# Four feed-forward stages of a two-layer hybrid block: weight-block sums by adding transfers, low parts by VectorE

## The chip, the cores and the metric

The kernel runs on one core of a Trainium2 chip. A core has five engines with a queue of instructions each: TensorE (PE: matmuls, with PEld its weight loads), VectorE (DVE), ScalarE (ACT), GpSimd (POOL) and SyncE (SP, which here only starts transfers). Data lies in the on-chip SBUF (128 partitions), matmul results in PSUM banks of 512 fp32 columns, the weights in HBM. Transfers run on the core's sixteen DMA engines; SP starts plain ones, POOL starts those that add what they read to what stands at the destination.

The metric is the device time of one execution in microseconds (us); lower is better.

## The reference

Two layers with the width 1024 on 256 tokens. Each layer is feed-forward, mixer, feed-forward, with a residual and a layer norm behind each part; the mixer of the first layer is a hybrid of two recurrences, that of the second a sparse attention. The change touches the feed-forward alone:

```python
def swiglu(x, w_in, w_out):
    gate, up = jnp.split(x @ w_in, 2, axis=-1)
    return (jax.nn.silu(gate) * up) @ w_out
...
    for layer in range(DEPTH):
        i = layer // 2
        h = layer_norm(DEEPNORM_ALPHA * h + 0.5 * swiglu(h, ffn_w_in[layer, 0], ffn_w_out[layer, 0]),
                       ln_g[layer, 0], ln_b[layer, 0])
        ...
        h = layer_norm(DEEPNORM_ALPHA * h + mix, ln_g[layer, 1], ln_b[layer, 1])
        h = layer_norm(DEEPNORM_ALPHA * h + 0.5 * swiglu(h, ffn_w_in[layer, 1], ffn_w_out[layer, 1]),
                       ln_g[layer, 2], ln_b[layer, 2])
```

w_in is 1024 x 5632 (gate and up, 2816 columns each), w_out 2816 x 1024, all fp32. There are four feed-forward parts.

## The kernel before

**Two halves of each number.** A matmul runs on operands rounded to a shorter form (F32R). To keep fp32's accuracy each operand is split in a high part, the rounded value, and a low part, the value less the high part. A product is then three matmuls: high by high, low by high, high by low (`mm3`, line 818). Weights are split as they arrive (`halved`, line 676): ScalarE copies the 128x1024 tile to `whi`, VectorE subtracts it from `raw` into `wlo`. One tile is 512 KB.

**A feed-forward stage** (`ffn`, line 1044). The 2816 inner columns are done in eleven steps of 256. Steps 0 to 2 are plain products. The other eight steps are four *chunks* of 512 columns, each by seven products of half-size blocks instead of eight (`wide`, line 751): gate and up, the two halves of the 1024 rows and the two halves of the 256 tokens make 2 x 2 blocks; with sums of blocks on both sides seven products do. The token sums are made once a stage (`token_forms`, line 734). The sums on the weights' side are made in every chunk:

| product | weight block | made from |
|---|---|---|
| a | b11 | loaded |
| b | b11 + b12 | b, in b11's tiles |
| d | b11 + b12 + b22 | d, in b11's tiles |
| e | b12 + b22 | e, in b12's tiles |
| g | b22 | loaded |
| c | b21 | loaded |
| f | b11 + b12 + b22 + b21 | f, in b11's tiles |

A block is two tiles of 128x1024 (256 rows by 512 columns), so each of the four sums is two additions on VectorE (`add`, line 758), 128 in the program. A product is twelve matmuls of 512 columns into a bank named `ps` or `mp` (b and g).

**The second matrix.** As inner columns get ready, their rows of w_out are loaded (`weights_to`, line 1094, and `rows`, line 705) and multiplied into four banks `acc`, twelve matmuls for each 128 inner columns (`out_mm`, line 1061). These row terms are placed between the products of the chunks (`flush`, with the counts in `TERMS`). For rows 8, 10, ... 20 of each stage (`ADDED`, line 55; 28 in all) `rows` makes the low part without VectorE: ScalarE writes the negated rounded value to `wlo`, and a transfer started by POOL adds the weights from HBM to it once more.

**The order.** The kernel is written as a list of operations with their data dependences. A planner (`Plan.order`, line 352) turns the whole program, all six stages, into one fixed order for each engine before anything runs. It goes by a price for each operation, by the place in the list as priority, by a rate for the transfers, and by the tiles: 52 tiles of 4 KB a partition for everything, of which the stream "W" (weights: `raw`, `whi`, `wlo`) may hold 14 or 28. At run time an engine takes its instructions in that order and each waits for the semaphores of what it needs. All instructions bear the line 561, where the order is emitted, so groups are told apart by the names of their tiles.

**Stages in time.** Feed-forward 1 from 0 to about 187 us, the hybrid mixer to about 420, feed-forward 2 to about 600, feed-forward 3 to about 776, the sparse attention to about 900, feed-forward 4 to the end.

Of the kernel before, what the change touches and what calls it, by code (L numbers as in the profile page):

```python
# [10 lines left out]
F32R = mybir.dt.float32r  # L11
I32 = mybir.dt.int32
AF = mybir.ActivationFunctionType
OP = mybir.AluOpType
# [37 lines left out]

TERMS = ((0, 1, 1, 1, 1, 1, 1), (0, 0, 1, 1, 1, 1, 0), (0, 0, 1, 1, 1, 1, 0), (0, 0, 1, 1, 1, 0, 0))

ADDED = range(8, 22, 2)

STRANDS = ("mp",)
W_HYB, W_NSA = (60.0, 140.0, 25.0, 40.0, 15.0), (70.0, 60.0, 40.0, 20.0)
# [8 lines left out]
def H3(t, h):  # L67
    return t.rearrange("p (h t) -> p h t", h=h)
# [118 lines left out]
class Plan:  # L187
# [25 lines left out]
    def add(self, eng, fn, args, kw, alts=None):  # L213
        op = Op()
        op.eng, op.fn, op.args, op.kw, op.idx = eng, fn, args, kw, len(self.ops)
        op.prio = op.idx + self.base
        op.alts = alts
        op.deps, op.succ, op.alloc, op.nbytes = {}, [], None, 0
        if self.gate is not None:
            op.deps[self.gate] = True  # L220
        op.tiles = []
        writes, reads = [], []
        for n, a in enumerate(args):
            if isinstance(a, V):
                (writes if n == 0 else reads).append(a)
        for k, a in kw.items():
            if isinstance(a, V):
                (writes if k == "accum_out" else reads).append(a)
        seen = set()
        for a, w in [(a, False) for a in reads] + [(a, True) for a in writes]:  # L230
            t = a.t
            psum = t.space == "PSUM"
            if psum:
                p0, p1, at = 0, 128, None
            else:
                p0, p1, at = a.p0, a.p1, np.zeros(int(np.prod(t.shape[1:])), bool)
                at[a.ids] = True
            if not t.acc:
                assert w, (t.name, fn)
                t.order = op.idx  # L240
            keep = []
            held = False
            for x in t.acc:
                o, xw, a0, a1, xat = x
                hit = a0 < p1 and p0 < a1 and (at is None or bool((at & xat).any()))
                if hit and (w or xw) and o is not op:
                    op.deps[o.idx] = held = True
                if not (w and hit and p0 <= a0 and a1 <= p1 and (at is None or not (xat & ~at).any())) or o is op:
                    keep.append(x)
            keep.append((op, w, p0, p1, at))  # L250
            t.acc = keep
            if not held and id(t) not in seen:
                op.alloc = (op.alloc or []) + [t]
            if id(t) not in seen:
                seen.add(id(t))
                op.tiles.append(t)
                t.left += 1
        if TRACE is not None:
            TRACE(op, args)
        self.ops.append(op)  # L260
        return op
# [323 lines left out]
class K:  # L585
# [116 lines left out]

        return [(hi[:, e, :], lo[:, e, :]) for hi, lo in self.tiled(srcs, k) for e in range(hi.shape[1])]

    def rows(self, w, f, added=False):

        nc = self.nc
        raw = self.arrive(w[f])
        if not added:
            return self.halved(raw)  # L710
        hi, lo = self.m4(1024, "whi", "W", F32R), self.m4(1024, "wlo", "W", F32R)
        nc.scalar.activation(lo, raw, AF.Copy, scale=-1.0)
        nc.gpsimd.dma_start(lo, w[f], accum_op=OP.add)
        nc.scalar.activation(hi, raw, AF.Copy)
        return hi, lo

    def first_weights(self, w, n0, arrivals):

# [32 lines left out]
    def wide(self, w, n0, forms, gout):  # L751

        nc, V = self.nc, self.nc.vector

        def load(block):
            return [self.arrive(w[n0 + 2 * block + e]) for e in range(2)]

        def add(out, a):
            for e in range(2):
                V.tensor_tensor(out[e], out[e], a[e], OP.add)  # L760

        def product(bank, name, src, start, stop):
            ah, al = forms[name]
            on = {} if start and stop else dict(skip_group_check=True)
            mm = nc.tensor.matmul
            for e in range(2):
                wh, wl = (H3(t, 2) for t in self.halved(src[e]))
                for k in range(2):
                    n = 2 * e + k
                    mm(bank, ah[n], wh[:, k], start=start and n == 0, stop=False, **on)  # L770
                    mm(bank, al[n], wh[:, k], start=False, stop=False, **on)
                for k in range(2):
                    n = 2 * e + k
                    mm(bank, ah[n], wl[:, k], start=False, stop=n == 3, **on)

        r, q = self.bank("ps"), self.bank("mp")
        s, t, u, v = (H3(self.m4(1024, n, "F"), 2)[:, e] for n in ("su", "vg") for e in range(2))
        b11 = load(0)
        product(r, "a", b11, True, False)
        nc.scalar.activation(s, r, AF.Copy)  # L780
        yield
        b12 = load(1)
        add(b11, b12)
        product(q, "b", b11, True, False)
        yield
        b22 = load(2)
        add(b11, b22)
        product(r, "d", b11, False, False)
        nc.scalar.activation(t, r, AF.Copy)
        yield  # L790
        add(b12, b22)
        product(r, "e", b12, False, False)
        nc.scalar.activation(v, r, AF.Copy)
        V.tensor_tensor(v, q, v, OP.subtract)
        yield
        product(q, "g", b22, False, True)
        V.tensor_tensor(u, q, t, OP.subtract)
        yield
        b21 = load(3)
        p = self.bank("ps")  # L800
        product(p, "c", b21, True, True)
        V.tensor_tensor(s, p, s, OP.add)
        nc.scalar.activation(s, s, AF.Silu)
        V.tensor_tensor(u, s, u, OP.mult)
        yield
        add(b11, b21)
        product(r, "f", b11, False, True)
        nc.scalar.activation(t, r, AF.Silu)
        V.tensor_tensor(v, t, v, OP.mult)
        gh, gl = gout  # L810
        for b, g in enumerate((u, v)):
            pt = self.bank("mp")
            for f in range(4):
                nc.tensor.transpose(pt[:, f * P:(f + 1) * P], g[:, f * P:(f + 1) * P], self.ident)
            self.split(gh[:, :, b * P:(b + 1) * P], gl[:, :, b * P:(b + 1) * P], H3(pt, 4))
        yield
# [227 lines left out]
    def ffn(self, l, j, x, then, last=False):  # L1044
        nc = self.nc
        w_in = self.i['ffn_w_in'][2 * l + j]
        w_out = self.i['ffn_w_out'][l, j].rearrange("(k p) n -> k p n", p=P)
# [44 lines left out]
        terms, late, wos = [], [], []  # L1092

        def weights_to(n):
            while len(wos) < min(n, NF):
                wos.append(self.rows(w_out, len(wos), len(wos) in ADDED))

        def flush(most):
            for f, g in [terms.pop(0) for _ in range(min(most, len(terms)))]:
                weights_to(f + AHEAD)  # L1100
                out_mm(0, f, g, wos[f])
                if count[0, 0] > NF - LAG - (3 if last else 0):
                    late.append((f, g, wos[f]))
                else:
                    out_mm(1, f, g, wos[f])
# [3 lines left out]
        for s in range(NT, steps):  # L1109
            wg, wu = (self.col_tiles([w_in[8 + 4 * (s - NT) + 2 * n + e] for e in range(2)]) for n in range(2))  # L1110
            self.mark = len(self.plan.ops) - 1
            for e in range(2):
                f = 2 * s + e
# [8 lines left out]
                if s == NT and e == 0:  # L1122
                    forms = self.token_forms(x)
        weights_to(AHEAD)
        for n in range(CHUNKS):
            f0 = 2 * steps + 4 * n
# [76 lines left out]
    def rates(self, pg):  # L1203

        nc = self.nc
        self.ncs = self.sm([P, 48], "ncs")
        nc.scalar.activation(self.ncs, pg[:, :48], AF.Copy, scale=-1.0)
        pt = self.bank("mp")
        nc.tensor.transpose(pt[:48, :P], self.ncs, self.ident)
        rows = self.sm([48, P], "ncsT")  # L1210
        self.copy(rows, pt[:48, :P])
        self.caps.setdefault("rows", (1, "DRAM"))
        self.cum = self.plan.tile("rows", [48, P], F32, "rows", space="DRAM")
        nc.sync.dma_start(self.cum, rows)
# [1024 lines left out]
```

## Time and profile before

| | us |
|---|---|
| median of 3 runs | 1086.62 |
| lowest and highest | 1086.55, 1088.65 |
| the profiled execution | 1087.19 |
| its span, first to last instruction | 1085.5 |

The page gives the busy time of each engine, the transfers by queue (q1 is SP's, q0 POOL's), the chain of work that ended last, and the costliest groups of instructions. A group's row has the line, the engine, the operation, the tile written and those read, shapes and count; behind the bar the busy time in us, the mean of one in ns, and the idle time of the engine just before, with what ended it. The granted clock of TensorE was 0.995 of full speed. A matmul of 512 columns shows about 390 ns from its start to its end, but the next one starts 227 ns after it, since they are pipelined: the pace is read from the starts.

### The profile page before, as it was taken

What the parts mean: (1) busy time and instruction counts of PE and PEld (TensorE: products, weight loads), DVE (VectorE), ACT (ScalarE), POOL (GpSimd) and SP (SyncE); (2) the same over time, 40 slices, a digit from 0 to 9 for tenths busy, and PEclk for the clock granted to TensorE, in tenths of its full rate; (3) what the DMA queues carried; (4) which work ended last, traced back from release to release, by engine and by line L of the source; (5) the groups of instructions that cost most, each with busy time, mean ns of one, the idle gap of its engine ahead of it and who ended that gap; (6) DMA issues with size and microseconds to landing.
All of it is one profiled execution on the core that took longest, in us unless ns stands there. A gap on an engine that the chain in (4) does not pass through costs nothing.

```text
span 1085.5 us, 16212 instructions
## 1 busy us (share of the span) xinstructions
PE 1066.3 (98%) x5946; PEld 893.3 (82%) x5946; DVE 1010.9 (93%) x1453; ACT 725.9 (67%) x1155; POOL 70.7 (7%) x116
## 2 busy tenths in 40 slices
PE   8999999998999999999999999999999999999997
PEld 6788888897999788888888888888887778888886
DVE  7999999799979999999999999999978889999995
ACT  7767866368737774667866667678465778666780
POOL 1000000001001310000000000000001000000000
PEclk9999999999999999999999999999999899999999
DMA  8658768535433575367777736679563336457881
GB/s 330 231 196 256 221 233 284 179 135 182 140 115 99 194 269 180 117 230 251 215 229 254 257 125 215 235 241 303 189 214 98 92 123 216 152 188 236 255 231 41
DMA packets 65034, 215.71 MB, mean 199 GB/s; under 512 B 8301, under 2 KB 12218, under 8 KB 64954
## 3 DMA queue, kind: packets, MB, share of 16 engines
q1 hardware_dynamic: 60922, 199.98, 52.8%
q0 software_dynamic: 4032, 14.68, 7.2%
q8 instruction: 47, 0.77, 0.3%
q14 instruction: 33, 0.27, 0.1%
HBM read 211.86 MB, written 1.07 MB: 196 GB/s over the span
## 4 chain that ended last, share of the span: by engine, by line
PE 84%; DVE 12%; ACT 1%; DMA 1%; issue 1%; POOL 0%; SPq 0%; DVEq 0%; ACTq 0%
PE ps L561 39%; PE acc L561 31%; PE mp L561 14%; DVE wlo L561 2%; DVE cv L561 2%; DVE arena L561 1%; DMA raw<-in_ffn_w_in_dram 1%; DVE o L561 1%; DVE sw L561 1%; DVE x L561 1%; DVE y L561 1%; DVE qs L561 1%; DVE AT L561 0%; POOL arena L561 0%; DVE Y L561 0%
## 5 line engine op out<-in xcount | busy, mean ns | idle before, releaser
L561 ACT ACTIVATE whi<-raw 128x1024 fp32r<-128x1024 f32 (+1 forms) x435 | 436.8, 1052 | 104.0 <-DVE raw L561 85.4
L561 DVE TENSOR_TENSOR wlo<-raw,whi 128x1024 fp32r<-128x1024 f32 (+2 forms) x419 | 491.4, 1205 | 7.1 <-ACT whi L561 6.1
L561 PE MATMUL ps<-whi,x 128*128 128x512 f32 (+1 forms) x864 | 234.8, 390 | 0.3 <-ACT cv L561 0.3
L561 PEld LDWEIGHTS ps<-whi,x 128*128 128x128 f32 x864 | 156.7, 188 | 30.6 <-issue 1.5
L561 DVE TENSOR_TENSOR raw<-raw,raw 128x1024 f32<-128x1024 f32 x128 | 152.8, 1216 | 0.0
L561 PE MATMUL ps<-wlo,x 128*128 128x512 f32 (+1 forms) x432 | 127.1, 385 | 0.0
L561 PE MATMUL ps<-x,whi 128*128 128x256 f32 (+2 forms) x560 | 114.3, 312 | 4.0 <-ACT cv L561 2.4
L561 PEld LDWEIGHTS ps<-x,whi 128*128 128x128 f32 (+1 forms) x560 | 90.4, 188 | 11.4 <-ACT cv L561 3.8
L561 PE MATMUL acc<-whi,gh 128*128 128x512 f32 x253 | 99.3, 393 | 0.0
L561 PE MATMUL acc<-wlo,gh 128*128 128x512 f32 x253 | 99.0, 391 | 0.0
L561 PE MATMUL acc<-whi,gl 128*128 128x512 f32 x253 | 97.9, 390 | 0.0
L561 PEld LDWEIGHTS ps<-wlo,x 128*128 128x128 f32 x432 | 79.6, 188 | 15.3 <-issue 0.4
L561 PE MATMUL ps<-x,wlo 128*128 128x256 f32 (+1 forms) x344 | 80.0, 284 | 0.5 <-DVE wlo L561 0.5
L561 PE MATMUL acc<-whi,x 128*128 128x512 f32 x224 | 73.7, 405 | 2.3 <-DVE x L561 0.8
L561 PE MATMUL acc<-whi,g 128*128 128x512 f32 x192 | 63.3, 392 | 0.0
L561 POOL DMA_DIRECT2D wlo<-in_ffn_w_out_dram x28 | 24.4, 872 | 569.2 <-ACT wlo L561 391.3
L561 PEld LDWEIGHTS ps<-x,wlo 128*128 128x128 f32 (+1 forms) x344 | 58.1, 189 | 2.1 <-DVE wlo L561 0.7
L561 PEld LDWEIGHTS acc<-whi,gl 128*128 128x128 f32 x253 | 47.5, 188 | 9.8
L561 PEld LDWEIGHTS acc<-whi,gh 128*128 128x128 f32 x253 | 47.5, 188 | 9.5
L561 PEld LDWEIGHTS acc<-wlo,gh 128*128 128x128 f32 x253 | 47.5, 188 | 9.5
L561 PEld LDWEIGHTS acc<-whi,x 128*128 128x128 f32 x224 | 41.8, 189 | 11.8 <-ACT whi L561 2.1
L561 PE MATMUL mp<-whi,fhi 128*128 128x512 f32 x128 | 49.9, 390 | 0.0
(284 smaller groups left out, 1735.2 us busy)
## 6 DMA issues: line engine op xcount, KB each, us to landing
raw<-in_ffn_w_in_dram SPq DMA_DIRECT2D x174, 512.0 KB, 5.5
raw<-in_ffn_w_out_dram SPq DMA_DIRECT2D x88, 512.0 KB, 3.7
wlo<-in_ffn_w_out_dram POOLq DMA_DIRECT2D x28, 512.0 KB, 8.5
raw<-in_hyb_w_col_dram SPq DMA_DIRECT2D x28, 512.0 KB, 4.5
raw<-in_hyb_w_tok_dram SPq DMA_DIRECT2D x16, 512.0 KB, 7.8
raw<-in_hyb_w_out_dram SPq DMA_DIRECT2D x16, 512.0 KB, 3.7
raw<-in_nsa_w_tok_dram SPq DMA_DIRECT2D x8, 512.0 KB, 6.6
raw<-in_nsa_w_one_dram SPq DMA_DIRECT2D x8, 512.0 KB, 5.8
```

The costliest lines, as they stand in the source:

```text
L561: r = getattr(getattr(nc, eng), fn)(*[res(a) for a in args], **{k: res(a) for k, a in kw.items()})
```

## The change

The sums e and f of each chunk are no longer made by VectorE. A transfer started by POOL adds the block b22 from HBM to the tiles of b12 (sum e), and block b21 to the tiles of b11 (sum f). It is placed in the list as soon as the tile's earlier value isn't needed any more: e right behind sum b, f right behind product d. The blocks b22 and b21 are still loaded for their own products. In turn the second matrix's rows all get their low part from VectorE, and `ADDED` goes.

```diff
-ADDED = range(8, 22, 2)
+SUMS = ("e", "f")
...
-    def rows(self, w, f, added=False):
-
-        nc = self.nc
-        raw = self.arrive(w[f])
-        if not added:
-            return self.halved(raw)
-        hi, lo = self.m4(1024, "whi", "W", F32R), self.m4(1024, "wlo", "W", F32R)
-        nc.scalar.activation(lo, raw, AF.Copy, scale=-1.0)
-        nc.gpsimd.dma_start(lo, w[f], accum_op=OP.add)
-        nc.scalar.activation(hi, raw, AF.Copy)
-        return hi, lo
+    def rows(self, w, f):
+
+        return self.halved(self.arrive(w[f]))
...
-        def add(out, a):
+        def add(name, out, a, block):
             for e in range(2):
-                V.tensor_tensor(out[e], out[e], a[e], OP.add)
+                if name in SUMS:
+                    nc.gpsimd.dma_start(out[e], w[n0 + 2 * block + e], accum_op=OP.add)
+                else:
+                    V.tensor_tensor(out[e], out[e], a[e], OP.add)
...
         b12 = load(1)
-        add(b11, b12)
+        add("b", b11, b12, 1)
+        if "e" in SUMS:
+            add("e", b12, None, 2)
         product(q, "b", b11, True, False)
         yield
         b22 = load(2)
-        add(b11, b22)
+        add("d", b11, b22, 2)
         product(r, "d", b11, False, False)
+        if "f" in SUMS:
+            add("f", b11, None, 3)
         nc.scalar.activation(t, r, AF.Copy)
         yield
-        add(b12, b22)
+        if "e" not in SUMS:
+            add("e", b12, b22, 2)
         product(r, "e", b12, False, False)
...
-        add(b11, b21)
+        if "f" not in SUMS:
+            add("f", b11, b21, 3)
         product(r, "f", b11, False, True)
...
-                wos.append(self.rows(w_out, len(wos), len(wos) in ADDED))
+                wos.append(self.rows(w_out, len(wos)))
```

## The prediction

> **What bounds the kernel now.** I read the page first (engine shares, the chain of work that ended last), then the windows of the four feed-forward stages, then the chain inside one chunk, and last the waits.
>
> ```profile
> PE 1066.3 (98%) x5946; PEld 893.3 (82%) x5946; DVE 1010.9 (93%) x1453; ACT 725.9 (67%) x1155; POOL 70.7 (7%) x116
> PE 84%; DVE 12%; ACT 1%; DMA 1%; issue 1%; POOL 0%; SPq 0%; DVEq 0%; ACTq 0%
> ```
>
> TensorE (PE) is busy 98% of the span and holds 84% of the chain. VectorE (DVE), the engine that the change relieves, holds 12%. A share over the span doesn't say where, so the next view takes the stretch of the four chunks in each of the four feed-forward stages. Its columns are the length, the busy time of PE, weight loads, DVE, ACT and POOL, each with its count, then the granted clock, the DMA share and GB/s.
>
> ```profile
> 50.00:176.00 126.00, 126.00 (x573) 104.35 (x572) 124.56 (x124) 92.65 (x109) 6.19 (x7) 1.00 0.75 238
> 460.00:586.00 126.00, 126.00 (x573) 104.18 (x572) 123.12 (x124) 91.64 (x108) 6.09 (x7) 1.00 0.76 243
> 636.00:764.00 128.00, 128.00 (x581) 105.97 (x580) 125.82 (x145) 91.84 (x111) 6.02 (x7) 1.00 0.74 244
> 940.00:1068.00 128.00, 128.00 (x581) 105.79 (x580) 123.33 (x128) 88.02 (x104) 6.59 (x8) 1.00 0.68 210
> sum 508.00, PE 508.00 PEld 420.30 DVE 496.82 ACT 364.15 POOL 24.89; mean PE 127.00 PEld 105.08 DVE 124.21 ACT 91.04 POOL 6.22
> ```
>
> Two engines are full here: TensorE for 508.00 of 508.00 us, VectorE for 496.82. Which of them sets the pace? A matmul's end is modelled, so "busy" could hide waits of TensorE. The chain inside a chunk decides that: it lists starts, and a product is always twelve matmuls.
>
> ```profile
> 537.03 2.72 PE ps L561 x12
> 539.75 2.72 PE acc L561 x12
> 542.47 2.72 PE mp L561 x12
> 545.19 2.72 PE acc L561 x12
> 547.91 2.72 PE ps L561 x12
> 550.63 2.72 PE acc L561 x12
> 553.35 2.72 PE ps L561 x12
> ```
>
> Every twelve take 2.72 us, 0.227 us for each matmul, and the next twelve start in the same hundredth. Products of the first matrix (ps, mp) and row terms of the second (acc) alternate without a gap. The chain has nothing but PE in it. So TensorE sets the time of these stages at an even pitch, and VectorE, although full, keeps up. ScalarE does wait for VectorE's sums, 85.4 us of the 104.0 that it stands idle before the high copies (last two columns), and nobody behind it is late:
>
> ```profile
> L561 ACT ACTIVATE whi<-raw 128x1024 fp32r<-128x1024 f32 (+1 forms) x435 | 436.8, 1052 | 104.0 <-DVE raw L561 85.4
> ```
>
> **The change part by part.** The rows with the prices:
>
> ```profile
> L561 DVE TENSOR_TENSOR raw<-raw,raw 128x1024 f32<-128x1024 f32 x128 | 152.8, 1216 | 0.0
> 530.87 4.63 DVE L561 TENSOR_TENSOR wlo<-raw,whi 128x1024 fp32r<-128x1024 f32 x4
> L561 ACT ACTIVATE wlo<-raw 128x1024 fp32r<-128x1024 f32 x28 | 29.5, 1055 | 0.0
> q1 hardware_dynamic: 60922, 199.98, 52.8%
> q0 software_dynamic: 4032, 14.68, 7.2%
> DMA to landing us min/median/max: 5.4/8.5/11.2
> ```
>
> *Sums e and f.* There are 128 sums of blocks on VectorE: 4 stages x 4 chunks x 4 sums x 2 tiles. Half of them, 64, go. One lasts 1216 ns, but the starts of a run lie closer: (4.63 - 1.22) / 3 = 1.14 us. 64 x 1.14 = 73 us of VectorE go.
>
> *Low parts of the second matrix.* Rows 8, 10, ... 20 of each stage, 28 in all, lose the scaled copy on ScalarE (29.5 us) and the adding transfer, and get a subtraction of the same shape on VectorE: 28 x 1.14 = 32 us come back. Net VectorE: 73 - 32 = 41 us less, about 2.6 us for each of the 16 chunks. ScalarE: 29.5 us less.
>
> *What that is worth.* Nothing, by the chain above: the matmuls stay the same in number and shape, and they already follow each other at 0.227 us. The cover is TensorE itself. If it were gone, and VectorE set the pace, the 41 us would show (a rival below).
>
> *Adding transfers.* 28 go, 64 come: 36 more, 9 more in each stage. In the queue rows 28 transfers hold the sixteen DMA engines for 7.2% of 1085.5 us, so one takes 0.072 x 1085.5 / 28 = 2.79 us of all sixteen, where a plain load of the same 512 KB takes 0.528 x 1085.5 x 0.524 / 199.98 = 1.50 us. Nine more are 25.1 us a stage. Free DMA time in the four stretches: 126 x 0.25 = 31.5, 126 x 0.24 = 30.2, 128 x 0.26 = 33.3, 128 x 0.32 = 41.0 us. It fits, with 5 to 16 us left; the mean share rises to about 0.95, 0.96, 0.94 and 0.88. No row shows such a load kept up for 126 us. The nearest is the last chunk of the second stage, and the tight places are found by chunk:
>
> ```profile
> 50.00:80.00 30.00, 30.00 (x136) 24.85 (x135) 29.93 (x30) 19.65 (x24) 0.00 (x0) 1.00 0.63 205
> 460.00:490.00 30.00, 30.00 (x134) 24.76 (x133) 29.95 (x31) 18.06 (x21) 0.00 (x0) 1.00 0.62 211
> 554.00:586.00 32.00, 32.00 (x151) 26.46 (x150) 29.71 (x31) 26.69 (x33) 2.58 (x3) 1.00 0.95 299
> ```
>
> In 554 to 586 us the share is 0.95, three adding transfers are among it (the POOL count), and TensorE loses nothing. That row is nearest to what every chunk will look like, so I take the cost of the added traffic as zero; its other end, loads that come late, is priced under the rivals. The first chunks go from none to four transfers: 0.62 + 4 x 2.79 / 30 = 0.99.
>
> *The new wait.* The copy of e's and f's high part now waits for a transfer in place of a sum. On ScalarE the later copies are queued behind it, VectorE's low parts wait for those, and TensorE for both. Is there room? VectorE's list of the chunk around 520 us has the sums in the order b, b, e, d, d, e, f, f:
>
> ```profile
> 531.82 2.72 PE ps L561 x12
> 515.86 1.21 DVE L561 TENSOR_TENSOR raw<-raw,raw 128x1024 f32<-128x1024 f32 x1
> 535.42 2.35 DVE L561 TENSOR_TENSOR raw<-raw,raw 128x1024 f32<-128x1024 f32 x2
> ```
>
> The second b sum ends at 515.86 + 1.21 = 517.1; from then e's transfer may run. Product e is the ps that starts at 537.03, and its high copy takes 1.05 us, so the room is 537.03 - 1.05 - 517.1 = 18.9 us. For f, the block is free once product d (the ps at 531.82) has both halves, at the latest when it ends, at 534.5; product f starts at 553.35: 553.35 - 1.05 - 534.5 = 17.8 us. An adding transfer landed after 8.5 us in the median and 11.2 at worst. They now come in pairs, one sharing the engines with the other: 11.2 + 2.79 = 14.0 us, an estimate. That leaves 3.8 us, so I take 0. The other end is a pair that is late by one transfer in each chunk, 16 x 2.79 = 45 us; the 3.8 us speak against it, and a part of it stands among the rivals.
>
> *Issues and queues.* The row of the issues on POOL:
>
> ```profile
> L561 POOL DMA_DIRECT2D wlo<-in_ffn_w_out_dram x28 | 24.4, 872 | 569.2 <-ACT wlo L561 391.3
> ```
>
> It issues 64 such transfers of 0.87 us for 28; in these stages it has only the two powers of a layer norm to do besides (7 or 8 counts a stretch), and it is 93% idle: 0. SP's loads are the same, in another order. The tiles: no buffer is held longer than before, since b12 and b11 wait for their product anyway; the seven rows a stage need their low tile later: 0, or slightly below.
>
> *Order elsewhere.* The planner writes one order for the whole program, so the two mixers may come out in another order though no line of theirs changed. The sign is open. I take 0 and keep 4 us to both sides, 3% of the 12% x 1085.5 = 130 us that VectorE holds of the chain, which lie nearly all outside the feed-forward chunks.
>
> **Sum.** 0 (sums) + 0 (low parts) + 0 (transfers) + 0 (waits) on the profiled execution: it took 1087.19 us, its span is 1085.5, and the median of the runs shown is 1086.62. I forecast 1087, between the two.
>
> **The rivals.**
>
> *VectorE sets the pace after all: 1046 us.* For it: 496.82 of 508.00 us busy, and ScalarE's 85.4 us of waiting for sums. TensorE would then be stretched unseen, and the 41 us come off: 1087 - 41 = 1046. Against it: the even 2.72 us. The Trainium skill ("Perfetto Trace Analysis", Identifying the Most-Contended Engine) warns that matmul busy time is no measure of headroom and wants the busy share of the weight loads instead. By that rule the 420.30 of 508.00 us would promise up to 88 us of room; the trace doesn't bear it out here, since the starts of the matmuls leave none.
>
> *The freed engines help the mixers: 1083 us.* VectorE enters the hybrid and the attention stage with less backlog, and the order turns out better by the 4 us above. For it: VectorE's part of the chain lies there. Against it: that part is made of chains of small operations, not of weights.
>
> *The transfers press on the loads: 1096 us.* Place: chunks whose share reaches 1, that is the four first ones (0.99 by the sum above) and the last ones of the second and third stage (0.95 + 2.79 / 32 = 1.04). Mechanism: a load that is queued with a pair of adding transfers lands 2 x 2.79 = 5.6 us later.
>
> ```profile
> 507.08 0.80 SPq L561 DMA_DIRECT2D raw<-in_ffn_w_in_dram  x2
> 514.12 1.22 DVE L561 TENSOR_TENSOR raw<-raw,raw 128x1024 f32<-128x1024 f32 x1
> raw<-in_ffn_w_in_dram SPq DMA_DIRECT2D x174, 512.0 KB, 5.5
> ```
>
> A load issued at 507.08 lands after the median 5.5 us at 512.6, and the sum that wants it starts at 514.12: 1.5 us of slack. VectorE's new 2.6 us a chunk can make up for a stall. It decides beyond 1.5 + 2.6 = 4.1 us; the excess of 5.6 is 1.5 us a chunk, 6 x 1.5 = 9 us: 1096. For it: there is no chunk left with a slack share. Against it: the 0.95 chunk above lost nothing.
>
> *The order of the mixers turns out worse: 1091 us,* by the same 4 us.
>
> *The change doesn't do what it says,* say because the planner moves other work to VectorE: then the time is the same 1087, and it counts there.
>
> **How the numbers follow.** No change 0.45; loads pressed 0.25; mixers worse 0.07; mixers better 0.20; VectorE's pace 0.03. 0.2% is about what a measurement of this kernel can tell from no change, 2.2 us. Slower 0.32, same 0.45, faster 0.23. The range must reach the mixers' cases and nearly all of the pressed loads: 1081 (two us below 1083) to 1097. It leaves out the 0.03 of VectorE's pace and some 0.15 of tails. The likeliest case's own range is 1084.5 to 1089.
>
> **What would show it.** The sums on VectorE at 64 in place of 128, its low parts at 28 more of the 128x1024 form, 64 transfers on POOL; VectorE's busy time in the four stretches down by some 41 us while TensorE stays at 2.72 us for twelve: right. A DMA share of 0.95 with TensorE still even: the traffic fits. Wrong: pieces of DMA, ACT or DVE in the chain within 50 to 176 us and its like (loads pressed), or chunks that follow each other faster than now (VectorE's pace). If the four stretches are unchanged and the time moves, it comes from the mixers' order.

## The result, and the profile after

| | before | after |
|---|---|---|
| median | 1087.05 us (1086.55 to 1088.65, 4 runs) | 1095.51 us (1094.72 to 1097.92, 4 runs) |
| the profiled execution | 1087.19 us | 1094.72 us |
| its span | 1085.5 us | 1093.0 us |

The ratio after to before is 1.0079, with a 95% interval of 1.0059 to 1.0099. The kernel is slower by some 8 us, although VectorE and ScalarE both have less to do. The page of after:

```profile
PE 1069.3 (98%) x5946; PEld 892.5 (82%) x5946; DVE 976.8 (89%) x1421; ACT 700.7 (64%) x1123; POOL 101.5 (9%) x152
q0 software_dynamic: 9216, 33.56, 17.3%
PE 81%; DVE 11%; DMA 4%; issue 2%; ACT 1%; POOL 1%; SPq 0%; DVEq 0%; POOLq 0%; ACTq 0%
L561 DVE TENSOR_TENSOR raw<-raw,raw 128x1024 f32<-128x1024 f32 x64 | 76.9, 1216 | 0.2
raw<-in_ffn_w_out_dram SPq DMA_DIRECT2D x88, 512.0 KB, 5.7
raw<-in_ffn_w_in_dram POOLq DMA_DIRECT2D x64, 512.0 KB, 7.2
```

The change does what it says: 64 sums in place of 128 on VectorE, 64 adding transfers. VectorE is 1010.9 - 976.8 = 34.1 us less busy, ScalarE 25.2. But TensorE's part of the chain has gone down from 84% to 81%, and transfers hold 4% of it where they held 1%. The same four stretches as before, with the same columns:

```profile
50.00:176.00 126.00, 124.43 (x563) 102.19 (x563) 117.88 (x118) 89.91 (x105) 11.19 (x13) 1.00 0.92 278
460.00:586.00 126.00, 125.91 (x568) 103.12 (x566) 115.67 (x115) 87.35 (x104) 11.25 (x13) 1.00 0.93 279
636.00:764.00 128.00, 126.27 (x576) 104.08 (x574) 119.80 (x137) 88.96 (x107) 11.95 (x14) 1.00 0.89 267
940.00:1068.00 128.00, 127.17 (x581) 104.52 (x580) 117.30 (x120) 86.30 (x104) 12.19 (x14) 1.00 0.87 249
sum 508.00, PE 503.78 PEld 413.90 DVE 470.64 ACT 352.53 POOL 46.58; mean PE 125.94 PEld 103.48 DVE 117.66 ACT 88.13 POOL 11.64
```

The DMA shares are 0.92, 0.93, 0.89 and 0.87, close to the 0.95, 0.96, 0.94 and 0.88 that were foreseen. TensorE, which was busy for all of the 508.00 us, now has holes: 503.78. VectorE is less busy than before (470.64 for 496.82), so it is not full. What do the holes wait for? The waits of after (total us, times, longest):

```profile
DVE wlo L561 <- ACT whi L561: 29.8, 31, 3.4
ACT whi L561 <- DMA raw<-in_ffn_w_in_dram: 22.8, 21, 3.0
ACT whi L561 <- DMA raw<-in_ffn_w_out_dram: 14.0, 11, 2.9
PE mp L561 <- DVE vg L561: 4.1, 5, 1.6
```

And the three of them that the waits of before have:

```profile
ACT whi L561 <- DMA raw<-in_ffn_w_in_dram: 7.3, 5, 2.2
DVE wlo L561 <- ACT whi L561: 6.1, 11, 1.2
ACT whi L561 <- DMA raw<-in_ffn_w_out_dram: 1.4, 2, 1.0
```

Transfers now hold up ScalarE's high copies for 36.8 us in all (8.7 before). The one with w_out is plain loads of rows, and it has grown tenfold. The name with w_in could be plain loads or adding transfers. The profile's view of each queue's transfers tells them apart: for SP's plain loads it lists these copies as waiting for 42.8 us (all weights of all stages), for GpSimd's adding transfers it lists nobody. VectorE waits for those copies, 29.8 us (6.1), and TensorE waits for VectorE's `vg`, which it never did. The name `mp` covers two things, product g and the transposes at the end of a chunk, which read `vg` too; of the 4.1 us, 3.7 are product g's. These are the rows of the first kind of matmul of products b and g, before and after:

```profile
L561 PE MATMUL mp<-whi,fhi 128*128 128x512 f32 x128 | 49.9, 390 | 0.0
L561 PE MATMUL mp<-whi,fhi 128*128 128x512 f32 x128 | 51.0, 398 | 3.7 <-DVE vg L561 3.7
```

How these waits hang together is seen in the chain at one such hole (start, length, what), with the loads that stand in it at three other holes:

```profile
55.23 8.45 DMA raw<-in_ffn_w_out_dram
...
63.76 1.07 ACT whi L561
...
64.86 0.55 DVE wlo L561
65.40 0.60 issue
66.00 0.69 DVE vg L561
...
66.74 1.43 PE mp L561 x5
...
709.24 7.47 DMA raw<-in_ffn_w_out_dram
...
738.31 9.43 DMA raw<-in_ffn_w_in_dram
...
1014.21 8.64 DMA raw<-in_ffn_w_out_dram
```

Read it from the end. The `mp` at 66.74 is product g. It adds to the bank that holds product b, and VectorE must first have read b out of that bank: this is `vg`, the subtraction of b from e. Before it, ScalarE must have copied e out of its bank, into a tile that is named `vg` too. Both engines take their instructions in a fixed order, and high and low parts of other tiles stand ahead of these two. The timelines of ScalarE and VectorE at that place (start, busy time, in brackets the idle time before):

```profile
62.57 2.25 ACT L561 ACTIVATE whi<-raw 128x1024 fp32r<-128x1024 f32 x2 [2.73 <-DMA raw<-in_ffn_w_in_dram]
64.73 0.58 ACT L561 ACTIVATE vg<-ps 128x512 f32<-128x512 f32 x1
...
63.66 2.42 DVE L561 TENSOR_TENSOR wlo<-raw,whi 128x1024 fp32r<-128x1024 f32 x2 [1.69 <-ACT whi L561]
66.00 0.68 DVE L561 TENSOR_TENSOR vg<-mp,vg 128x512 f32<-128x512 f32 x1
```

ScalarE stands idle for 2.73 us until a load of w_in lands; it was issued at 50.24 and took 12.3 us. Its high copy is the first of the two at 62.57. The second is that of a row of the second matrix, whose load took 8.45 us and landed at 63.68, just as the first copy ended. Behind them stands the copy of e, which ends at 65.31. VectorE makes the two low parts of the same tiles, 1.69 us idle before the first, then `vg`, and behind `vg` waits TensorE. So two late loads, one of each matrix, stop product g, though neither the copy of e nor `vg` reads these tiles. The chain shows only the later of the two; by these times, as an estimate, either alone would have stopped product g for nearly as long. The holes that end near 722 and 1028 us lead back in the chain to loads of w_out that took 7.47 and 8.64 us, the one that ends near 753 to a load of w_in that took 9.43. The median from issue to landing went from 3.7 to 5.7 us for the loads of w_out and from 5.5 to 5.9 for those of w_in.

Where do the 7.5 us of the span come in? GpSimd computes a small power in each layer norm; its second one closes a stage. The last such row in after's timeline of GpSimd:

```profile
1087.09 0.92 POOL L561 TENSOR_TENSOR lnve<-lnve,mhalf 128x1 f32<-128x1 f32 x1 [11.57 <-DVE lnve L561]
```

These are the starts (us) of the same mark at the end of each stage, for both kernels and for three of the experiments below:

| end of | before | after | 64 columns | 330 GB/s plan | before, 330 GB/s plan |
|---|---|---|---|---|---|
| feed-forward 1 | 192.63 | 192.85 | 191.40 | 194.00 | 198.21 |
| hybrid | 429.93 | 431.33 | 429.89 | 430.56 | 437.46 |
| feed-forward 2 | 605.18 | 607.97 | 606.70 | 605.37 | 612.85 |
| feed-forward 3 | 779.89 | 784.45 | 781.76 | 781.06 | 787.92 |
| attention | 908.87 | 914.10 | 911.53 | 909.91 | 921.85 |
| feed-forward 4 | 1079.59 | 1087.09 | 1082.81 | 1080.45 | 1091.31 |

After against before: of 7.5 us, 5.65 come in the four feed-forward stages (0.2, 1.4, 1.8, 2.3) and 1.85 in the two mixers, whose code is the same.

### The profile page after: what moved, and what is told of

The parts are those of the page before. It is cut to its first block, busy times and chain, and to the rows that moved or that the text cites. A ratio compares the mean times of both kernels' runs of the same rounds, so it can differ in the third digit from the quotient of the medians.

```text
span 1093.0 us, 16286 instructions
## 1 busy us (share of the span) xinstructions
PE 1069.3 (98%) x5946; PEld 892.5 (82%) x5946; DVE 976.8 (89%) x1421; ACT 700.7 (64%) x1123; POOL 101.5 (9%) x152
## 4 chain that ended last, share of the span: by engine, by line
PE 81%; DVE 11%; DMA 4%; issue 2%; ACT 1%; POOL 1%; SPq 0%; DVEq 0%; POOLq 0%; ACTq 0%
PE ps L561 38%; PE acc L561 30%; PE mp L561 14%; DVE wlo L561 3%; DMA raw<-in_ffn_w_out_dram 2%; DMA raw<-in_ffn_w_in_dram 2%; DVE arena L561 1%; DVE cv L561 1%; ACT whi L561 1%; DVE sw L561 1%; POOL arena L561 1%; DVE qs L561 1%; DVE x L561 0%; DVE raw L561 0%; DVE AT L561 0%
## 5 line engine op out<-in xcount | busy, mean ns | idle before, releaser
L561 DVE TENSOR_TENSOR wlo<-raw,whi 128x1024 fp32r<-128x1024 f32 (+2 forms) x447 | 524.5, 1206 | 33.1 <-ACT whi L561 29.8
L561 ACT ACTIVATE whi<-raw 128x1024 fp32r<-128x1024 f32 (+2 forms) x433 | 437.2, 1051 | 123.6 <-DVE raw L561 77.4
L561 PE MATMUL ps<-whi,x 128*128 128x512 f32 (+1 forms) x864 | 234.0, 389 | 0.3 <-ACT cv L561 0.3
L561 PEld LDWEIGHTS ps<-whi,x 128*128 128x128 f32 x864 | 156.8, 188 | 30.4 <-issue 1.5
L561 PE MATMUL ps<-wlo,x 128*128 128x512 f32 (+1 forms) x432 | 127.2, 385 | 0.0
L561 PE MATMUL ps<-x,whi 128*128 128x256 f32 (+2 forms) x560 | 114.5, 312 | 4.0 <-ACT cv L561 2.4
L561 PEld LDWEIGHTS ps<-x,whi 128*128 128x128 f32 (+1 forms) x560 | 90.2, 188 | 11.2 <-ACT cv L561 3.8
L561 POOL DMA_DIRECT2D raw<-in_ffn_w_in_dram x64 | 55.6, 873 | 469.0 <-DVE raw L561 193.2
L561 PE MATMUL acc<-whi,gl 128*128 128x512 f32 x253 | 98.9, 392 | 0.0
L561 PE MATMUL acc<-wlo,gh 128*128 128x512 f32 x253 | 98.9, 391 | 0.0
L561 PE MATMUL acc<-whi,gh 128*128 128x512 f32 x253 | 98.4, 391 | 0.0
L561 PEld LDWEIGHTS ps<-wlo,x 128*128 128x128 f32 x432 | 79.6, 188 | 15.2 <-issue 0.4
L561 PE MATMUL ps<-x,wlo 128*128 128x256 f32 (+1 forms) x344 | 79.9, 284 | 0.4 <-DVE wlo L561 0.4
L561 DVE TENSOR_TENSOR raw<-raw,raw 128x1024 f32<-128x1024 f32 x64 | 76.9, 1216 | 0.2
L561 PE MATMUL acc<-whi,x 128*128 128x512 f32 x224 | 74.7, 408 | 1.8 <-DVE x L561 0.8
L561 PE MATMUL acc<-whi,g 128*128 128x512 f32 x192 | 63.8, 392 | 0.0
L561 PEld LDWEIGHTS ps<-x,wlo 128*128 128x128 f32 (+1 forms) x344 | 58.2, 189 | 2.0 <-DVE wlo L561 0.6
L561 PEld LDWEIGHTS acc<-whi,gh 128*128 128x128 f32 x253 | 47.5, 188 | 9.7
L561 PEld LDWEIGHTS acc<-wlo,gh 128*128 128x128 f32 x253 | 47.5, 188 | 9.7
L561 PEld LDWEIGHTS acc<-whi,gl 128*128 128x128 f32 x253 | 47.5, 188 | 9.5
L561 PE MATMUL mp<-whi,fhi 128*128 128x512 f32 x128 | 51.0, 398 | 3.7 <-DVE vg L561 3.7
L561 PEld LDWEIGHTS acc<-whi,x 128*128 128x128 f32 x224 | 41.9, 190 | 11.1 <-ACT whi L561 1.6
```

The source lines that it names most:

```text
L561: r = getattr(getattr(nc, eng), fn)(*[res(a) for a in args], **{k: res(a) for k, a in kw.items()})
```

## Experiments

The theory: the bytes fit, but loads land later; a late load stops TensorE through the order of ScalarE and VectorE. The rivals: the new order of the program costs the time whatever the transfers do; or the path of e's and f's sums through a transfer is too slow.

### The same order with fewer bytes

In after's order each adding transfer moves only a part of its tile: 512 of the 1024 columns, or 64. The rest of the sum is left out, so the result is not the reference's. Nothing else differs: every instruction, wait and place stays.

```diff
+                if 'accum_op' in kw:
+                    args = (args[0][:, :512], args[1][:, :512])
```

> The order of the changed kernel on every engine is kept as it is; only each of the 64 adding transfers moves the first 512 of 1024 columns (so half of each sum e and f is left out, and the output is not the reference's). Theory A, the added traffic presses on the plain loads: DMA share in the four chunk stretches falls from about 0.90 to 0.80 or less, the plain loads of the second matrix land in about 4 us instead of 5.7, product g no longer waits for VectorE, and the time comes back by at least two thirds of the 8.5 us: 1086 to 1090. Theory B, the new order written by the planner is the worse one whatever the transfers cost: no change, 1094 to 1097.

> The changed kernel's order on every engine and all its waits; each of the 64 adding transfers moves 64 of 1024 columns (nearly all of sums e and f is left out, and the output is not the reference's). The added traffic is gone, also that of the 28 transfers of before. Theory A (traffic) with nothing else: ratio to before 1.000 or below, 1085 to 1088. Theory B (the new order has a cost of its own): the ratio stays where half the bytes left it, 1.0025, so 1090 to 1092.

Measured against before: 1091.07 us, 1.0025 (1.0015 to 1.0035) with 512 columns; 1090.14 us, 1.0020 (1.0011 to 1.0030) with 64. The first lies between the two theories, 1 us above the range of the first; the second lies in the range of the theory of the order. The sum of the four stretches with 512 columns, then stretches with 64, and with 64 the rows of product g and of the transposes (the two lines of the cut move L561 to L563):

```profile
sum 508.00, PE 505.45 PEld 418.18 DVE 469.56 ACT 351.81 POOL 46.96; mean PE 126.36 PEld 104.55 DVE 117.39 ACT 87.95 POOL 11.74
```

```profile
50.00:176.00 126.00, 126.00 (x573) 104.31 (x572) 118.48 (x118) 90.36 (x106) 11.52 (x14) 1.00 0.70 224
460.00:586.00 126.00, 124.89 (x565) 103.14 (x565) 115.36 (x116) 86.91 (x102) 11.09 (x13) 1.00 0.68 225
sum 508.00, PE 506.17 PEld 418.70 DVE 469.16 ACT 350.68 POOL 46.74; mean PE 126.54 PEld 104.67 DVE 117.29 ACT 87.67 POOL 11.68
```

```profile
L563 PE MATMUL mp<-whi,fhi 128*128 128x512 f32 x128 | 49.8, 389 | 0.0
L563 PE MATMUL mp<-ident,vg 128*128 128x128 f32 x128 | 19.2, 272 | 1.8 <-DVE vg L563 1.8
```

With 64 columns product g no longer waits for `vg`, 0.0 for 3.7 us; with 512 columns it doesn't either. The load of w_in that took 12.3 us at the first hole takes 4.4, the row behind it 3.5 for 8.45, and the loads of w_out at the holes near 722 and 1028 take 3.4 and 3.5 for 7.47 and 8.64. ScalarE copies e at 63.24 us, as soon as product e is done. The instructions and their order are the same, so it is the bytes that make these loads late and product g wait.

What is left is another wait: TensorE stands still for 1.11 us near 583 and 0.72 us near 760, where transposes wait for `vg` with nearly no bytes in the adding transfers. Before has no such hole, so these belong to the new order.

So the time splits in two. The bytes cost 1.0079 - 1.0020 = 0.0059, 6.4 us (with both intervals, some 0.004 to 0.008); by the marks of the profiled executions it is 1087.09 - 1082.81 = 4.3 us. Of these, 1.45, 1.42 and 1.71 us come in the feed-forward stages 1, 3 and 4, and 0.2 us or less in each other stage. The order itself costs 0.0020, 2.2 us (3.2 us by the marks, 2.0 of it in the mixers and 1.6 in the second feed-forward stage; the first gains 1.2). The kernel with 64 columns has less traffic than before (0.70 for 0.75 in the first stretch), the one with 512 has more (0.82), so the price of the traffic that the change adds lies near these 6 us as well.

Half the bytes already give back 0.0054 of the 0.0059, nearly all (3.5 of the 4.3 us by the marks). So the cost doesn't grow evenly with the bytes, which fits a slack in the order: it begins where the loads are later than that slack.

### Traffic alone, in the order of before

Two kernels keep before's code and order and only add 64 transfers of 512 KB. In one, SP copies each tile of b22 and b21 from HBM to a scratch place in HBM, right behind its load (16 chunks x 2 blocks x 2 tiles = 64):

```diff
+                if extra:                       # loads of b22 and b21
+                    nc.sync.dma_start(away, args[1])
```

> The kernel before with its own order; behind each of the 128 plain loads of blocks b22 and b21 in the chunks... 64 tile loads in each half, SP starts a copy of the same 512 KB from HBM to a scratch place in HBM. Nobody waits for them and no tile is held. Theory A: the share in the chunk stretches rises to 0.90 or more, ScalarE's high copies wait for plain loads, product g for VectorE, and the time is 1092 to 1105. Theory B (only the order matters): 1086 to 1090.

Measured: 1099.42 us, 1.0100 (1.0086 to 1.0113), 10.9 us, as the theory of the traffic expected; the shares, 0.87, 0.83, 0.78 and 0.79, stay below the expected 0.90. The third stretch, and the wait:

```profile
636.00:764.00 128.00, 124.94 (x560) 102.31 (x559) 122.53 (x139) 89.61 (x106) 6.01 (x7) 0.99 0.78 272
```

```profile
PE mp L561 <- DVE vg L561: 5.3, 4, 2.5
```

The wait that before lacked, `mp` for `vg` (4.8 us of it product g's), is here with no change of the order of before. More traffic is enough to make it. The copies also stand in SP's queue ahead of later loads, so this kernel can't tell the engines' time from the queue's.

In the other, GpSimd stores each finished tile of the sums e and f to HBM:

```diff
+                if extra:                       # the additions of sums e and f
+                    nc.gpsimd.dma_start(away, res(args[0]))
```

> The order of the kernel before is kept on TensorE, VectorE, ScalarE and SP; behind each of the 64 additions e and f POOL starts a plain transfer of the summed tile to a scratch place in HBM (512 KB each, 64 x 1.50 = 96 us of all sixteen engines, against 36 x 2.79 = 100 us that the change added). Nobody reads what is stored; only the reuse of the tile waits for it. Theory A (traffic): the share in the chunk stretches rises from 0.73 to about 0.92, loads land late, 1092 to 1100. Theory B (order): 1086 to 1089, as before.

Measured: 1122.02 us, 1.0319 (1.0294 to 1.0345), far more than either theory had. Its third stretch:

```profile
636.00:764.00 128.00, 123.70 (x560) 101.71 (x559) 120.52 (x135) 84.44 (x103) 12.01 (x19) 0.97 0.73 248
```

The granted clock is 0.97 here where before had 1.00, and the stores stand in GpSimd's queue ahead of the rows' adding transfers and read tiles that must not be overwritten until they are done. Three things differ at once, so the run says nothing on the price of traffic.

### Parts of the change

`SUMS` is `("f",)`, `("e",)` or empty; all rows of the second matrix take VectorE's low part in each.

> Only sum f by adding transfers (32), sum e by VectorE again, the second matrix's low parts all by VectorE; the planner writes its own order. 32 adding transfers for the 28 of before, VectorE 32 sums less and 28 low parts more (4 x 1.14 = 5 us less), ScalarE 29.5 us less. Theory A: DMA share about 0.75, time as before, 1085 to 1089. Theory B: an order of its own, anywhere in 1084 to 1097; the share of DMA tells nothing.

> Only sum e by adding transfers (32), f by VectorE, the second matrix's low parts by VectorE. The same traffic as with f alone, where the time was 1.0019 of before. Theory A: 1087 to 1091, like f alone. If the short room between sum b and product e is what hurts, e alone is the worse one: 1092 to 1096.

> No adding transfers at all: sums on VectorE as in the kernel before, and the second matrix's 28 low parts on VectorE too (the second half of the change alone). DMA share falls to about 0.57, VectorE gets 32 us more where it had 11 us free in the four stretches. Theory A says that loads are early, so what is lost comes from VectorE alone: 1087 + (32 - 11) = 1108, with TensorE waiting for VectorE's low parts. If VectorE had more room than its busy share shows, 1088 to 1095.

| by adding transfer | median, us | ratio (95%) | shares in the four stretches |
|---|---|---|---|
| f | 1089.94 | 1.0019 (1.0007 to 1.0032) | .79 .78 .77 .70 |
| e | 1089.35 | 1.0015 (1.0006 to 1.0024) | .77 .78 .76 .68 |
| neither | 1102.50 | 1.0135 (1.0117 to 1.0154) | .63 .58 .55 .52 |
| both (after) | 1095.51 | 1.0079 (1.0059 to 1.0099) | .92 .93 .89 .87 |

Either sum alone, with half the transfers, costs 1.6 or 2.1 us, about what after's order cost with nearly no bytes; f alone lies 1 us above its expected range, e alone inside. Product g waits for `vg` for 1.0 us in each of the two. Both together cost 8.6, not 3.7: the parts don't add up, which fits a slack that is used up. It isn't shown by these runs alone, for each has an order of its own, and VectorE is nearly as busy as before in both (498.18 and 495.75 of 508.00 us). Neither e nor f is the culprit by itself. The kernel with neither:

```profile
sum 508.00, PE 506.78 PEld 418.34 DVE 506.50 ACT 327.37 POOL 0.00; mean PE 126.69 PEld 104.58 DVE 126.63 ACT 81.84 POOL 0.00
```

Without adding transfers VectorE is busy for 506.50 of 508.00 us, and the time is 14.7 us longer, somewhat less than the 1108 us expected. So the sums couldn't simply have stayed on VectorE beside all the low parts. That VectorE is the bound of the chunks there isn't shown: TensorE stands still for only 1.22 us in these stretches, and by the marks 7.2 of 13.9 us come in the mixers.

### The plan's rate for transfers

The planner counts on 380 GB/s. Planned with a lower rate it expects every load later, and puts the work that waits for loads later too. Code and bytes are after's (the line that turns the moved bytes into an end has the same edit).

```diff
-                    room = (155e3 if at < 8000.0 else 190e3) - moved.get(n, 0)
+                    room = (155e3 if at < 8000.0 else 165e3) - moved.get(n, 0)
```

> The changed kernel, planned with a slower rate of the transfers (330 GB/s where the planner went by 380; the loads of before ran at 349 while the queue was busy). Every instruction is the same, only the order may differ. Theory A in the form that loads come later than the plan says: an order that expects this takes back a part, 1088 to 1093. If the engines' capacity itself is short, no order helps: 1095 to 1100.

Measured with 330 GB/s: 1087.43 us, 1.0000 (0.9991 to 1.0009). The whole 8 us are back, more than the part that was expected. The shares (0.91, 0.92, 0.91, 0.80) and the landing (both medians 6.0 us, for 5.9 and 5.7 in after) show that the loads are no earlier; only the last stretch has a lower share. Yet TensorE is full again. The third stretch and the sum:

```profile
636.00:764.00 128.00, 128.00 (x582) 105.85 (x581) 118.26 (x136) 88.49 (x108) 11.10 (x13) 1.00 0.91 273
...
sum 508.00, PE 508.00 PEld 419.94 DVE 459.45 ACT 340.91 POOL 45.72; mean PE 127.00 PEld 104.99 DVE 114.86 ACT 85.23 POOL 11.43
```

ScalarE and VectorE at the place of the hole shown above:

```profile
63.50 0.60 ACT L561 ACTIVATE vg<-ps 128x512 f32<-128x512 f32 x1 [2.95 <-PE ps L561]
...
64.13 0.69 DVE L561 TENSOR_TENSOR vg<-mp,vg 128x512 f32<-128x512 f32 x1 [1.69 <-ACT vg L561]
65.08 2.36 DVE L561 TENSOR_TENSOR wlo<-raw,whi 128x1024 fp32r<-128x1024 f32 x2 [0.26 <-ACT whi L561]
```

The places have changed on both engines: the copy of e and `vg` come first, the high copies and the low part that waits for them after. In this kernel's chain product g starts at 66.19, right behind twelve matmuls that began at 63.47, on the beat of 2.72. The loads are as late as in after by their medians; what stands behind them has changed.

By the marks, 6.6 us come back, 3.9 in the feed-forward stages and 2.7 in the mixers, where no chunk is. The first stage has lost its hole of 1.57 us and still ends 1.15 us later than in after: elsewhere in it the new order costs more. So the recovery is more than the end of these holes.

Is the rate a cure, then? Four more kernels try it: after planned with 348, 410 and 300 GB/s, and before planned with 330.

> The changed kernel planned with 348 GB/s, about what plain loads ran at while the queue was busy in the kernel before (349). Theory A: between the two neighbours, 1087 to 1092. Theory C: anywhere in 1085 to 1097.

> The changed kernel planned with 410 GB/s, faster than anything measured here. Theory A: at least as slow as the change as made, 1095 to 1103, with product g waiting for VectorE. Theory C: anywhere in 1085 to 1097.

> The changed kernel planned with 300 GB/s for the transfers (330 gave 1.000 of before, 380 gave 1.008). Theory A, in its sharper form: the change costs time only where the plan expects transfers earlier than they land; then a still more cautious plan keeps the gain, 1085 to 1090. Theory C, the 330 order was a lucky one among orders that all scatter by some 4 us: anywhere in 1085 to 1097, not ordered by the rate.

> The kernel before, planned with 330 GB/s. Its transfers have slack as it is and TensorE loses nothing in the chunks, so theory A expects no gain from caution: 1085 to 1089. If the cautious plan helped any kernel by itself (better orders in the mixers), it would be faster than before by some us, 1080 to 1084, and the recovery under the change would be no answer to its transfers.

| kernel, rate | median, us | ratio (95%) | PE in the four stretches |
|---|---|---|---|
| after, 300 | 1110.74 | 1.0204 (1.0188 to 1.0220) | 505.63 |
| after, 330 | 1087.43 | 1.0000 (0.9991 to 1.0009) | 508.00 |
| after, 348 | 1091.75 | 1.0028 (1.0016 to 1.0039) | 508.00 |
| after, 380 | 1095.51 | 1.0079 (1.0059 to 1.0099) | 503.78 |
| after, 410 | 1101.95 | 1.0121 (1.0106 to 1.0137) | 501.12 |
| before, 330 | 1096.84 | 1.0081 (1.0068 to 1.0094) | 508.00 |

From 330 to 410 the time rises with the rate, as the theory of the late loads expected. Product g waits for `vg` neither at 330 nor at 348, for 3.7 us at 380, and at 410 for 5.4:

```profile
L561 PE MATMUL mp<-whi,fhi 128*128 128x512 f32 x128 | 51.2, 400 | 6.5 <-DVE vg L561 5.4 <-ACT whi L561 0.8
```

At 300 both theories missed: they had 1085 to 1097. This is the slowest of the five plans of after. 543 matmuls start in its first stretch where 573 did in before, and by the marks 19.9 of the 23.5 us that it loses come in the feed-forward stages; product g waits for no `vg` there, the transposes do for 2.1 us, and what costs the rest isn't known. The kernel before was expected at 1085 to 1089, or faster. Its four stretches were full already, and it loses 8.8 us by the plan that gives after 8 us back. Its chain at the first layer norm and the marks in the table of stages show where:

```profile
189.43 1.99 DVE h L561 x3
...
191.56 0.64 PE mp L561 x4
```

TensorE waits for VectorE's `h` at the layer norm, and this first stage ends at 198.21 for 192.63 us; the attention stage takes 921.85 - 787.92 = 133.9 us for 129.0 by the marks. So a new order can move the time by several us outside the chunks. That limits what the 330 GB/s run proves: the holes of the chunks are gone, which its stretches show (4.2 us of TensorE); that the remaining some 4 us come from the same cause isn't shown, and the 2.7 us in the mixers speak against it. At 348 the stretches are full and 3 us remain; its profiled execution took 1088.80 us, among the lowest of its runs, so its trace can't tell where the others spent them. None of these kernels is faster than before.

## Why the prediction was right or wrong

The forecast was no change, 1087, and the kernel is 0.8% slower. The likeliest case was wrong. The time lies in the range, next to the rival named "The transfers press on the loads: 1096 us".

**The bound: right.** TensorE set the pace of the chunks before, and still does wherever nothing is late. VectorE's relief is worth nothing: 34.1 us less of it (41 foreseen) and 25.2 us less of ScalarE (29.5 foreseen) bought no time. The kernel with 64 columns shows it best: it has the relief and nearly no bytes in the adding transfers, and its ratio is 1.0020. VectorE's pace as a rival is refuted.

**Traffic: the sizes were right, the price was not.** One adding transfer holds the sixteen engines for 0.173 x 1093.0 / 64 = 2.95 us (2.79 foreseen), and the shares of the stretches came out within 0.05 (that of the first chunk did not: 0.87, 0.99 foreseen). The failed step is the sentence "I take the cost of the added traffic as zero". Its own sign of being wrong, pieces of DMA, ACT and DVE in the chain between 50 and 176 us, came. The bytes cost 6.4 us by the medians of after and of the kernel with 64 columns, 4.3 us by their marks. What the runs showed in its place: product g waits 3.7 us for `vg`, behind high copies and low parts of loads that land late, and 0.0 us with the same order and fewer bytes. The step rested on one stretch, 554 to 586 us, with a share of 0.95 and no loss. Two rows of after show why that stretch was no measure for the others:

```profile
50.00:80.00 30.00, 28.43 (x125) 23.20 (x125) 27.41 (x29) 19.64 (x22) 2.57 (x3) 1.00 0.87 261
...
554.00:586.00 32.00, 31.93 (x147) 25.90 (x145) 29.71 (x31) 24.98 (x30) 1.75 (x2) 1.00 0.99 325
```

The chunk that was taken as the measure now has a share of 0.99 and still loses next to nothing, 0.07 us. The first chunk has only 0.87 and loses 1.57 us; with half of the bytes and the same order it has 0.85 and loses nothing. The share of the engines doesn't say which load is late, nor who stands behind it.

**The new wait of e and f: right.** The adding transfers landed after 7.2 us in the median and 10.6 at most, within the room of 17.8 and 18.9 us; the estimate of 14.0 for a pair was too high. In the second chunk of the first stage GpSimd's timeline has the second issue of e:

```profile
75.76 0.86 POOL L561 DMA_DIRECT2D raw<-in_ffn_w_in_dram  x1 [0.19 <-issue]
```

and the chain has product e, twelve matmuls `ps`:

```profile
95.23 2.72 PE ps L561 x12
```

By the longest landing e is there at 75.76 + 10.6 = 86.4 us, nearly 9 us before its product. For all sixteen chunks the list of who waited for the tiles of the adding transfers is empty in after, where the plain loads have 42.8 us. So the rival that the sums' path through a transfer is too slow falls too.

**The rival's mechanism: right in kind, wrong in place.** Loads landed later and the lateness reached TensorE, as the rival said. But it put the place at b's sum, with 1.5 us of slack, in chunks whose share reaches 1. The sums on VectorE were idle for 0.2 us in all before their 64 (the row of the first page above). The late loads, of both matrices, reached TensorE through the high copies on ScalarE and the low parts on VectorE that stand ahead of the copy of e and of `vg`. The prediction named this very path, ScalarE's later copies, VectorE's low parts and TensorE, for the transfers of e and f, where it cost nothing; it didn't follow it from a late plain load, nor ask what else stands behind the waiter. Its 9 us agree with the result partly by chance: 6.4 us are the bytes' and 2.2 the order's.

**Order elsewhere: inside its bound.** Taken as 0 with 4 us to both sides, it is 0.0020, 2.2 us (0.0011 to 0.0030), with the 2.0 us of the mixers by the marks. The sum had no term for the order inside the feed-forward stages, where transposes came to wait for `vg`. The bound would have been too narrow for another rate of the plan: before planned with 330 GB/s lost 8.8 us.

**Still open.** How much of the recovery at 330 GB/s comes from the holes and how much from the luck of another order, and where the 3 us at 348 GB/s lie. What costs most of the loss at 300 GB/s is open too. Moving the copy of e and `vg` ahead of the high and low parts by hand, all else fixed, was not tried; moving `vg` alone could have won at most some 0.7 us of the 1.57 at the first hole, for the copy of e ended at 65.31 and `vg` began at 66.00.

## What to carry to other kernels

A share of the DMA engines below 1 says that the bytes fit, not that each load is in time: here 0.87 cost TensorE 1.57 us in one chunk and 0.99 cost 0.07 us in another. Before calling added traffic free, take each load that may land later, find the engine that waits for it, and read what stands behind that wait in the engine's order, also for other reasons, and on the next engine too; the bound engine may wait for one of those. Where a fixed order is planned with a rate, a change of the traffic is worth a plan with another rate: here five rates moved the same instructions by up to 23 us. A change of some us in such a kernel needs a run with the same order and fewer bytes before it is put down to either.

## What the runs showed of the hardware

The engine that was relieved is the one that TensorE now waits for: with VectorE busy for 496.82 of 508.00 us TensorE did not wait for it in these stretches; with 470.64 it does, since VectorE now stands idle until late loads have landed and been copied, and does afterwards what TensorE needs.

An adding transfer doesn't cost in proportion to its bytes. From the queue rows of the three kernels with one order, 0.173 x 1093.0 / 64, 0.097 x 1089.5 / 64 and 0.022 x 1088.7 / 64 give 2.95 us of the sixteen engines for 512 KB, 1.65 for 256 KB and 0.37 for 32 KB: a sixteenth of the bytes takes an eighth of the time.

A copy from HBM to HBM holds the engines for less than a load of the same size, by an estimate, and yet 64 of them cost about as much as the whole change:

```profile
q1 hardware_dynamic: 62970, 233.54, 58.2%
```

Before, this row has 52.8% of 1085.5 us. (0.582 x 1098.2 - 0.528 x 1085.5) / 64 is about 1.03 us for each copy, an estimate that lets the loads cost what they did; a load of 512 KB took 1.50. The kernel lost 10.9 us by them.
